# Group 1's triangular inversion moved to VectorE, and the opening of the recurrence emitted in another order

## The chip, the cores and the metric

The kernel runs on one core of one Trainium2 chip. The metric is the device time of one execution in microseconds (us); lower is better. Engines are named as in the profile: PE (TensorE's matmuls), DVE (VectorE), ACT (ScalarE), POOL (GpSimd) and SP (SyncE, which here issues most DMA transfers).

## The reference

Two layers of a diffusion transformer block over 512 latent and 256 context tokens of width 1024. Each layer projects the normed input; one part of the columns feeds a bidirectional RWKV recurrence of 8 heads of 64, the other a differential attention of 8 heads; their outputs are concatenated and projected, and a squared-ReLU MLP follows. What matters here is the recurrence:

```
def wkv_scan(state0, r, w, k, v, kk, b, reverse):
    xs = tuple(jnp.swapaxes(t.astype(jnp.float32), 0, 1) for t in (r, w, k, v, kk, b))

    def step(state, inp):
        r_t, w_t, k_t, v_t, kk_t, b_t = inp
        sa = jnp.einsum("bhvk,bhk->bhv", state, kk_t)
        state = (state * w_t[:, :, None, :]
                 - sa[..., :, None] * b_t[:, :, None, :]
                 + v_t[..., :, None] * k_t[:, :, None, :])
        y = jnp.einsum("bhvk,bhk->bhv", state, r_t)
        return state, y
```

It runs forward and backward, first over the context, then from the context's state over the latent tokens.

## The kernel before

The recurrence is computed in chunks of 64 tokens. Two chunks of 64 make a group of 128 tokens; there are 6 groups, and each is treated in both directions (d = 0 and 1) at once. Per group there are three kinds of work.

*Preparation.* `prep_a` and `prep_b` handle a unit of one group, one direction and half of the heads: 24 units per layer, in the order of the groups. A unit loads the projected columns (L973), makes decay and rate with a small matmul (L977) and a tanh on ACT (L982), doubles it to sg on POOL (L1014), takes a running sum over the chunk on DVE (L1018 forward, L1020 backward), exponentials on ACT, and writes scaled keys (BK, L1034 and L1035). Matmuls of these (L1046) are masked on DVE (L1048) into S, the chunk's matrices, and the keys are transposed (L1053). `preps()` gives out the units one after the other; when the fourth unit of a group is done, the group's number is put into `ready`.

*Inversion.* Each chunk's unit triangular 64x64 matrix has to be inverted. `relay` copies the two diagonal 32x32 blocks of every matrix to DRAM (L1086), `inv` loads them back as N and W (L1115, L1116), `eliminate` inverts all of a group's blocks together in 30 sweeps of one multiplication (L1100) and one addition (L1102) each, 60 instructions one behind the other, and after that the inverse goes out to DRAM as it is (dn, L1123) and transposed (dt, through R, L1125 and L1127), and back as TT (L1132) and into S (L1137). `merge` then makes the off-diagonal block with 32 small matmuls on PE (L1152, L1154), a copy Z on ACT, 32 more matmuls (L1160, L1162), and a copy into S on DVE (L1164) and one on ACT (L1165).

*Steps.* `step(n, j)` advances the recurrence by one chunk in both directions: it loads the values uv (L1176), multiplies keys and state into X (L1186, L1189), copies that to xs (L1192), solves with the inverse into us (L1198), updates the state with more matmuls (L1210) and two DVE instructions (L1213, L1215), and makes the output y (L1226). Every step needs the merged inverse of its group from L1198 on.

The attention of the layer (`phase_wr`: row maximum L797, exponential L799, scaling by the second softmax L809, transposes L815 and their copies L820, values L832, norm L843 and L848, store L858) runs while the first units are prepared. Its loop calls `side(1)` after its pieces, which emits the next piece of `prologue()`. What the prologue has not emitted when attention is through is drained by `rest()`, which then does merge(0), merge(1) and the steps, and between their parts emits the later groups' preparation and inversion and the rows of the adaptive norm for the rest of the layer (`ada`, weights loaded by L254 into raw, multiplied by L265).

The order on each engine is made by a scheduler at build time from the order of emission, dependences and its own estimates, so an instruction can stand before or behind its neighbours of emission. Each engine then works through its own order strictly: an instruction that waits holds up what is behind it. This holds for SP's transfers as well.

Before the change, groups 0 and 1 are eliminated on POOL (`n < 2`) and groups 2 to 5 on DVE, and the prologue emits all units of groups 0 and 1, then all of inv(0), then all of inv(1).

Of the kernel before, what the change touches and what calls it, by code (L numbers as in the profile page):

```python
# [10 lines left out]
F32 = mybir.dt.float32  # L11
# [153 lines left out]
class K:  # L165
# [760 lines left out]
    def recurrence(self, l, last, es, side):  # L926

        nc, tc, I, dr = self.nc, self.tc, self.I, self.dr
        tp = self.pool(es, "tp", 1)
        iv = self.pool(es, "iv", 1)  # L930
# [128 lines left out]
        def preps():  # L1059
            todo = [(n, d, pp) for n in range(6) for d in range(2) for pp in (0, 2)]  # L1060
            nxt = prep_a(*todo[0])
            for i, it in enumerate(todo):
                cur = nxt
                if i + 1 < len(todo):
                    nxt = prep_a(*todo[i + 1])
                yield
                yield from prep_b(*it, *cur)
                if it[1:] == (1, 2):
                    ready.append(it[0])
                    yield  # L1070

        ready, tts = [], {}
        prepg = preps()
# [15 lines left out]
        def base(d, bl):  # L1089
            b = (bl + d) % 2 * 32 + d * 16  # L1090
            return slice(b, b + 16)

        def eliminate(N, W, n):

            for t in range(1, 31):
                k, w = (t + 1) // 2, 31 - t
                pr = iv.tile([128, 128], F32, name=self.n("pr"), tag=f"pr{n < 2}")
                prv = pr[:, 0:k * w].rearrange("p (s j) -> p s j", s=k)
                ve = nc.gpsimd if n < 2 else nc.vector
                ve.tensor_tensor(prv, W[:, 0:k, t:t + 1].to_broadcast([128, k, w]),  # L1100
                                        N[:, t:t + 1, t + 1:32].to_broadcast([128, k, w]), ALU.mult)
                ve.tensor_tensor(W[:, 0:k, t + 1:32], W[:, 0:k, t + 1:32], prv, ALU.add)  # L1102
                if t % 4 == 0:
                    yield
            for par in range(2):
                nc.gpsimd.memset(W[64 * par:64 * par + 64].rearrange("p s t -> p (s t)")[:, par:512:34], 1.0)

        def inv(n):

            N = iv.tile([128, 32, 32], F32, name=self.n("N"), tag="N", bufs=2)  # L1110
            W = iv.tile([128, 16, 32], F32, name=self.n("W"), tag="W", bufs=2)
            da = das[n].rearrange("u (i r t) -> u i r t", r=2, t=32)
            for par in range(2):
                ps = slice(64 * par, 64 * par + 64)
                nc.sync.dma_start(W[ps], da[:, :, par])  # L1115
                nc.sync.dma_start(N[ps].rearrange("p s t -> p (s t)"), das[n])  # L1116
            yield
            yield from eliminate(N, W, n)
            dn = dr.tile([64, 1024], F32, name=self.n("dn"))
            dt_ = dr.tile([32, 2, 512], F32, name=self.n("dt"))  # L1120
            dv = dn.rearrange("u (i r t) -> u i r t", r=2, t=32)
            for par in range(2):
                nc.sync.dma_start(dv[:, :, par], W[64 * par:64 * par + 64])  # L1123
            R = iv.tile([128, 32, 16], F32, name=self.n("R"), tag="R")
            nc.scalar.copy(R, W.rearrange("p s t -> p t s"))  # L1125
            for par in range(2):
                nc.sync.dma_start(dt_[:, par], R[64 * par:64 * par + 32].rearrange("p t s -> p (t s)"))  # L1127
            yield
            Gs = [sets[(n, d)][2].rearrange("s u h t -> s (u h) t") for d in range(2)]
            TT = iv.tile([64, 16, 32], F32, name=self.n("TT"), tag="TT")  # L1130
            for d in range(2):
                nc.sync.dma_start(TT[32 * d:32 * d + 32].rearrange("t u (r i) -> t (u r) i", r=2),  # L1132
                                  dt_[16 * d:16 * d + 16].rearrange("u r (t i) -> t (u r) i", t=32))
            for d in range(2):
                for bl in range(2):
                    bs = slice(32 * bl, 32 * bl + 32)
                    nc.sync.dma_start(Gs[d][bs, :, bs], dn[base(d, bl), :].rearrange("u (s t) -> s u t", s=32))  # L1137
            tts[n] = TT
            yield
            if n > 1:  # L1140
                merge(n)
                yield

        def merge(n):
            TT = tts.pop(n)
            Gs = [sets[(n, d)][2].rearrange("s u h t -> s (u h) t") for d in range(2)]
            a, e = slice(0, 32), slice(32, 64)
            get = late.get("pg", bank)
            zps = get([64, 16, 32])
            Z = iv.tile([64, 16, 32], F32, name=self.n("Z"), tag="Z")  # L1150
            for u in range(16):
                nc.tensor.matmul(zps[e, u, :], Gs[0][a, u, 32:64], TT[a, u, :],  # L1152
                                 start=True, stop=True, skip_group_check=True)
                nc.tensor.matmul(zps[a, u, :], Gs[1][e, u, 0:32], TT[e, u, :],  # L1154
                                 start=True, stop=True, skip_group_check=True)

            nc.scalar.copy(Z.rearrange("p u (i r) -> p u r i", r=2), zps.rearrange("p u (r i) -> p u r i", r=2))
            nps = get([64, 16, 32])
            for u in range(16):
                nc.tensor.matmul(nps[a, u, :], Z[e, u, :], Gs[0][e, u, 32:64],  # L1160
                                 start=True, stop=True, skip_group_check=True)
                nc.tensor.matmul(nps[e, u, :], Z[a, u, :], Gs[1][a, u, 0:32],  # L1162
                                 start=True, stop=True, skip_group_check=True)
            nc.vector.tensor_copy(Gs[0][a, :, 32:64], nps[a])  # L1164
            nc.scalar.copy(Gs[1][e, :, 0:32], nps[e])  # L1165
# [130 lines left out]
            yield  # L1296

        def prologue():
            while 1 not in ready:
                yield next(prepg)  # L1300
            yield from inv(0)
            yield from inv(1)

        def rest():
            nonlocal uvp, fp, px, us, xsd
# [50 lines left out]
        done, spare = [], []  # L1356
        uvp = fp = px = us = xsd = None
        side.add(prologue())
        return rest

# [379 lines left out]
```

## Time and profile before

| | |
|---|---|
| median of 3 runs | 2432.26 us (2419.16 to 2433.48) |
| the profiled execution | 2426.55 us, its span 2424.8 us |
| busy share of the span: PE, DVE, ACT, POOL | 93%, 63%, 48%, 33% |
| mean granted clock of TensorE | 0.946 of 2.4 GHz |

The span is the time from the first to the last instruction; it is taken from one execution. Busy time counts the time in which an engine runs an instruction, and not its waits. A granted clock of 1.00 is the full clock of TensorE and 0.5 half of it; a mean over a stretch lies between. A timeline row gives the start, the duration, the engine, the line of the kernel, the operation, what it writes and reads, the count of instructions that it stands for, and in brackets the idle time of the engine before it with what ended it.

### The profile page before, as it was taken

The numbers are of one execution on the slowest core, as the hardware profiler recorded it, in microseconds if no ns is written. First come the engines' busy times: TensorE is split into PE (matmuls) and PEld (weight loads), VectorE is DVE, ScalarE is ACT, GpSimd is POOL, SyncE is SP. The second block draws the span as 40 slices with busy tenths as digits, with TensorE's granted clock in tenths as the row PEclk, the third lists the DMA queues.
The fourth block names the chain that finished last, engine by engine and source line by source line (L and its number), as shares of the span: only waits on it lengthen the run. The fifth ranks groups of instructions, "written<-read, shape, count | busy, mean of one in ns | idle before, by whom it ended". The sixth has DMA issues, their size and how long they took to land.

```text
span 2424.8 us, 43738 instructions
## 1 busy us (share of the span) xinstructions
PE 2250.5 (93%) x17150; PEld 1903.9 (79%) x17150; DVE 1518.5 (63%) x2629; ACT 1174.4 (48%) x2393; POOL 803.6 (33%) x1048
## 2 busy tenths in 40 slices
PE   6999998899988999999999999999879988999997
PEld 5887887787777988888888887778767877788886
DVE  5456458647755675555556736665856575778784
ACT  4345547545534544333344435555735544555552
POOL 1212324832212343333330422323562121553530
PEclk9999999779998999999999999999879988999999
DMA  7543445377577521111112344454567664423230
GB/s 275 157 131 87 122 126 134 81 207 186 148 190 221 196 92 60 64 61 62 61 63 85 136 137 133 115 144 110 115 171 198 153 181 161 165 88 121 86 114 35
DMA packets 291630, 313.67 MB, mean 129 GB/s; under 512 B 139680, under 2 KB 220896, under 8 KB 291424
## 3 DMA queue, kind: packets, MB, share of 16 engines
q1 hardware_dynamic: 280320, 284.66, 38.8%
q0 software_dynamic: 10240, 23.08, 5.0%
q8 instruction: 135, 2.21, 0.4%
q10 hardware_dynamic: 864, 3.15, 0.3%
q14 instruction: 71, 0.58, 0.1%
HBM read 257.04 MB, written 53.77 MB: 128 GB/s over the span
## 4 chain that ended last, share of the span: by engine, by line
PE 66%; DVE 10%; DMA 8%; issue 5%; POOL 4%; ACT 4%; SPq 2%; ACTq 0%; POOLq 0%; DVEq 0%
PE pf L351 32%; PE pu L351 16%; PE po L351 4%; DMA raw<-in_ada_w 2%; PE po L832 2%; PE pb L1046 2%; PE sc L795 1%; DVE wl L1500 1%; POOL pr L1100 1%; POOL W L1102 1%; PE X L1189 1%; DVE nm L797 1%; PE X L1226 1%; PE adar L265 1%; PE ptr L815 1%
## 5 line engine op out<-in xcount | busy, mean ns | idle before, releaser
L1500 DVE TENSOR_TENSOR wl<-raw,wh 128x1024 fp32r<-128x1024 f32 x170 | 255.8, 1507 | 125.0 <-ACT wh L1499 124.2
L351 PE MATMUL pf<-hl,wh 128*128 128x512 f32 (+1 forms) x832 | 282.1, 342 | 0.0
L351 PE MATMUL pf<-hh,wh 128*128 128x512 f32 (+1 forms) x832 | 280.5, 342 | 0.6 <-ACT hh L397 0.6
L351 PE MATMUL pf<-hh,wl 128*128 128x512 f32 (+1 forms) x832 | 275.7, 342 | 0.0
L1499 ACT ACTIVATE wh<-raw 128x1024 fp32r<-128x1024 f32 x170 | 179.2, 1058 | 161.5 <-PE pf L351 143.9
L351 PE MATMUL pf<-wh,fah 128*128 128x512 f32 x570 | 224.5, 396 | 13.2 <-DVE fu L1633 7.2
L351 PE MATMUL pu<-hh,wh 128*128 128x512 f32 (+1 forms) x632 | 223.7, 354 | 4.8 <-DVE t L557 1.7
L351 PE MATMUL pf<-wl,fah 128*128 128x512 f32 x570 | 223.9, 394 | 0.7 <-DVE wl L1500 0.7
L351 PE MATMUL pf<-wh,fal 128*128 128x512 f32 x570 | 221.4, 394 | 1.8 <-DVE fal L1600 1.8
L351 PE MATMUL pu<-hh,wl 128*128 128x512 f32 (+1 forms) x632 | 218.6, 346 | 4.0 <-DVE wl L340 4.0
L351 PE MATMUL pu<-hl,wh 128*128 128x512 f32 (+1 forms) x632 | 218.0, 345 | 0.0
L797 DVE TENSOR_REDUCE nm<-sc 128x1 f32<-128x768 f32 (+1 forms) x160 | 132.5, 841 | 79.3 <-PE sc L795 78.5
L351 PEld LDWEIGHTS pf<-hl,wh 128*128 128x128 f32 x832 | 156.6, 188 | 20.0 <-DVE hl L399 0.2
L351 PEld LDWEIGHTS pf<-hh,wl 128*128 128x128 f32 x832 | 156.1, 188 | 20.0
L351 PEld LDWEIGHTS pf<-hh,wh 128*128 128x128 f32 x832 | 155.3, 188 | 20.4 <-ACT hh L397 0.8
L799 ACT ACTIVATE e<-sc,nm 128x768 f32<-128x768 f32 (+1 forms) x160 | 130.7, 821 | 53.9 <-DVE nm L797 44.3
L321 POOL TENSOR_TENSOR rs<-ms,pw 128x1 f32<-128x1 f32 (+2 forms) x60 | 56.7, 948 | 271.2 <-DVE ms L319 270.5
L351 PEld LDWEIGHTS pu<-hh,wh 128*128 128x128 f32 x632 | 121.2, 192 | 23.4 <-DVE t L557 2.4
L351 PEld LDWEIGHTS pf<-wh,fah 128*128 128x128 f32 x570 | 107.2, 188 | 40.6 <-ACT fah L1599 13.6
L1633 DVE TENSOR_TENSOR acc<-pf,acc 128x512 f32<-128x512 f32 x155 | 104.2, 682 | 53.9 <-PE pf L351 53.3
L351 PEld LDWEIGHTS pu<-hh,wl 128*128 128x128 f32 x632 | 121.0, 192 | 19.0 <-DVE wl L340 4.8
L351 PEld LDWEIGHTS pu<-hl,wh 128*128 128x128 f32 x632 | 121.1, 192 | 14.3 <-issue 1.7
(262 smaller groups left out, 5607.1 us busy)
## 6 DMA issues: line engine op xcount, KB each, us to landing
raw<-in_w_ff SPq DMA_DIRECT2D x128, 512.0 KB, 3.7
raw<-in_ada_w SPq DMA_DIRECT2D x96, 512.0 KB, 6.5
raw<-in_w_in SPq DMA_DIRECT2D x52, 512.0 KB, 4.0
ld<-zd SPq DMA_DIRECT2D x40, 384.0 KB, 5.5
ks<-qd POOLq DMA_DIRECT2D x64, 192.0 KB, 5.4
zd<-zr SPq DMA_DIRECT2D x22, 384.0 KB
raw<-in_w_out SPq DMA_DIRECT2D x16, 512.0 KB, 5.9
qs<-qd POOLq DMA_DIRECT2D x32, 192.0 KB, 5.9
```

The source lines that it names most:

```text
L265: nc.tensor.matmul(acc[32 * g:32 * g + 32, :], self.sc[:, 2 * kp + k, :], raw[:, k, g * 128:g * 128 + 128], start=(kp + k == 0), stop=(kp ...
L321: nc.gpsimd.tensor_tensor(r, m, self.pw1.to_broadcast([128, cols]), ALU.pow)
L351: nc.tensor.matmul(out, a, b, start=(start and i == 0 and j == 0), stop=(i == n - 1 and j == 2), skip_group_check=not start)
L795: nc.tensor.matmul(sc[:, k0:k1], qs[:, br, tk], ks[:, br, k0:k1], start=True, stop=True)
L797: nc.vector.tensor_reduce(nm, sc, AX.X, ALU.max, negate=True)
L799: nc.scalar.activation(ee, sc, AF.Exp, bias=nm, accum_out=ls[:, br:br + 1])
L815: nc.tensor.transpose(pt[:, (k - k0) * 128:(k - k0) * 128 + 128], e[0][:, k * 128:k * 128 + 128], self.ident)
L832: nc.tensor.matmul(po, pT[:, k * 128:k * 128 + 128], vn[:, k, h * 64:h * 64 + 64], start=(k == 0), stop=(k == nk - 1))
L1046: nc.tensor.matmul(pgt[:, u, 0:nn], BK[hs, u, :], KR[hs, 2 * pp + u, 0:nn], start=True, stop=True, skip_group_check=True)
L1499: nc.scalar.activation(hi, src, AF.Copy)
L1500: nc.vector.tensor_tensor(lo, src, hi.bitcast(F32), sub)
L1633: nc.vector.tensor_tensor(d, p, d, add)
```

## The change

Two edits in `recurrence()`. In `eliminate`, group 1's 60 instructions go to DVE instead of POOL, and its products pr use the buffer of the later groups. In `prologue`, the units are emitted until group 0 is ready; then one piece of preparation and one piece of inv(0) are emitted by turns until group 1 is ready, and then pieces of inv(1) and inv(0) by turns.

```
@@ eliminate
-                pr = iv.tile([128, 128], F32, name=self.n("pr"), tag=f"pr{n < 2}")
+                pr = iv.tile([128, 128], F32, name=self.n("pr"), tag=f"pr{n == 0}")
                 prv = pr[:, 0:k * w].rearrange("p (s j) -> p s j", s=k)
-                ve = nc.gpsimd if n < 2 else nc.vector
+                ve = nc.gpsimd if n == 0 else nc.vector
@@ prologue
-            while 1 not in ready:
+            while 0 not in ready:
                 yield next(prepg)
-            yield from inv(0)
-            yield from inv(1)
+
+            first, second = inv(0), None
+            while first or second or 1 not in ready:
+                if 1 not in ready:
+                    next(prepg)
+                    if 1 in ready:
+                        second = inv(1)
+                elif second and next(second, self) is self:
+                    second = None
+                    continue
+                if first and next(first, self) is self:
+                    first = None
+                yield
```

How the engines' orders differ after it is shown at three places. The first is SP's order in layer 0 at the end of attention (od is its last store; uv are the values of step (0,0) in the two directions; dn, dt, TT and S with these numbers are group 1's inverse; gprow and raw belong to the adaptive norm). It is a piece of the difference, with + for rows that only the changed kernel has here.

```order
 L858 DMA od_522<-oT_5103 128x768
 L1176 DMA uv_5296<-vnd_521 64x512
+L1123 DMA dn_4905<-W_4704 1024x1x32 x2
 L1176 DMA uv_5298<-vnd_521 64x512
+L1127 DMA dt_4906<-R_4909 32x512 x2
+L1137 DMA S_4141<-dn_4905 32x16x32 x2
+L1132 DMA TT_4928<-dt_4906 32x32x16 x2
+L1137 DMA S_4484<-dn_4905 32x16x32 x2
 L306 DMA gprow_5315<-in_rows 128x256
 L254 DMA raw_5318<-in_ada_w 128x1024
```

The ten transfers of group 1's inverse moved from a later place in the queue to between and behind the two uv loads, ahead of the loads of in_ada_w.

The second is PE's order in layer 0, from the end of merge(1)'s first half (TT_4928, Z_5227 and pg_5226 are its tiles; X_5407 and us_5152 belong to step (0,0); adar to the adaptive norm). It is again a piece of the difference.

```order
+L1154 MATMUL pg_5226<-TT_4928,S_4484 32x32
+L1189 MATMUL X_5407<-sbd_3609,S_3914 128x128
+L1198 MATMUL us_5152<-xs_5130,S_3658 64x64 x8
+L1053 MATMUL pb_5544<-cst,BK_5526 128x128 x4
+L977 MATMUL pb_5554<-ltz_3602,wab_3600 128x256
 L265 MATMUL adar_5317<-raw_5318,sc 32x128 x8
-L1189 MATMUL X_5407<-sbd_3609,S_3914 128x128 x3
-L1198 MATMUL us_5152<-xs_5130,S_3658 64x64 x2
+L1160 MATMUL pg_5261<-S_4141,Z_5227 32x32
```

Merge(1) moved ahead: its first half stands before the last matmul of X and the solve of step (0,0), its second half behind the first L265; before, both stood behind step (0,1)'s X.

The third is DVE's order in layer 1 around merge(0)'s copy L1164 (W_17731 is group 1's block, W_18643 group 2's). Before:

```order
L1032 SCALAR_TENSOR_TENSOR ta_18915<-ta_18915,ld_18909 128x256
L1035 TENSOR_TENSOR BK_19010<-th_18914,xi_19004 128x4x64
L1034 TENSOR_TENSOR BK_19010<-ta_18915,xi_19004 128x4x64
L1164 COPY S_16631<-pg_18205 32x16x32
L309 TENSOR_TENSOR row_18709<-adar_18668,gprow_18666 128x128
L310 TENSOR_TENSOR row_18709<-row_18709,gprow_18666 128x128
L1100 TENSOR_TENSOR pr_18714<-W_18643,N_18642 128x30
```

In the changed kernel, DVE has there:

```order
L1102 TENSOR_TENSOR W_17731<-W_17731,pr_17935 128x15
L1100 TENSOR_TENSOR pr_18714<-W_18643,N_18642 128x30
L1102 TENSOR_TENSOR W_18643<-W_18643,pr_18714 128x30
L1100 TENSOR_TENSOR pr_18717<-W_18643,N_18642 128x29
L1102 TENSOR_TENSOR W_18643<-W_18643,pr_18717 128x29
L1100 TENSOR_TENSOR pr_18720<-W_18643,N_18642 128x56
L1102 TENSOR_TENSOR W_18643<-W_18643,pr_18720 128x2x28
L1100 TENSOR_TENSOR pr_18723<-W_18643,N_18642 128x54
L1102 TENSOR_TENSOR W_18643<-W_18643,pr_18723 128x2x27
L1164 COPY S_16631<-pg_18205 32x16x32
```

Ahead of the copy there stand now the last instructions of group 1's elimination and the first eight of group 2's, which used to stand behind it. Elsewhere in layer 1, counting the units of both layers from 0 (24 to 27 are layer 1's group 0): eleven instructions of group 1's elimination stand on DVE ahead of the mask (L1048) of unit 34; on PE the last L832 of attention stands ahead of L977 of unit 32, and used to stand behind that of unit 33; and on POOL sg (L1014) of unit 38 stands ahead of the last instruction of group 0's elimination, and used to stand behind it.

## Rows read from the trace of the kernel before

**Rows 1.** The page: busy time of each engine, and the ending chain by line.

```profile
PE 2250.5 (93%) x17150; PEld 1903.9 (79%) x17150; DVE 1518.5 (63%) x2629; ACT 1174.4 (48%) x2393; POOL 803.6 (33%) x1048
PE pf L351 32%; PE pu L351 16%; PE po L351 4%; DMA raw<-in_ada_w 2%; PE po L832 2%; PE pb L1046 2%; PE sc L795 1%; DVE wl L1500 1%; POOL pr L1100 1%; POOL W L1102 1%; PE X L1189 1%; DVE nm L797 1%; PE X L1226 1%; PE adar L265 1%; PE ptr L815 1%
```

**Rows 2.** Layer 0: window, length, busy time (instructions) by engine, PE clock, DMA share, GB/s.

```profile
520.00:540.00 20.00, 19.27 (x307) 15.83 (x306) 6.18 (x13) 5.72 (x13) 2.36 (x5) 0.66 0.89 197
```

**Rows 3.** Windows of layer 1; engines in the order PE, PEld, DVE, ACT, POOL.

```profile
1740.00:1800.00 60.00, 43.25 (x495) 34.05 (x493) 30.80 (x59) 24.03 (x59) 45.78 (x110) 0.71 0.69 167
1800.00:1860.00 60.00, 55.42 (x826) 45.08 (x826) 40.37 (x119) 30.09 (x74) 17.62 (x45) 0.87 0.77 194
```

**Rows 4.** Groups of instructions: busy us, mean ns of one, idle before and its releaser.

```profile
L1100 DVE TENSOR_TENSOR pr<-W,N 128x30 f32<-128x30 f32 (+7 forms) x240 | 67.6, 282 | 31.9 <-DMA N<-da 26.6
L1102 DVE TENSOR_TENSOR W<-W,pr 128x30 f32<-128x30 f32 (+7 forms) x240 | 65.2, 272 | 5.8
L1102 POOL TENSOR_TENSOR W<-W,pr 128x30 f32<-128x30 f32 (+7 forms) x120 | 48.2, 402 | 7.9
L1100 POOL TENSOR_TENSOR pr<-W,N 128x30 f32<-128x30 f32 (+7 forms) x120 | 47.1, 393 | 12.8 <-DMA N<-da 3.8 <-issue 1.8
```

**Rows 5.** Timeline of SP's queue in layer 0 (SPq issues transfers).

```profile
465.29 1.27 SPq L1123 DMA_DIRECT2D dn<-W  x2
...
490.40 1.38 SPq L254 DMA_DIRECT2D raw<-in_ada_w  x3
...
504.81 2.08 SPq L1123 DMA_DIRECT2D dn<-W  x2
```

**Rows 6.** Timeline of PE in layer 0.

```profile
472.37 0.31 PE L1152 MATMUL pg<-TT,S 32*32 32x32 f32 x2 [0.71 <-DMA TT<-dt]
...
500.64 0.64 PE L265 MATMUL adar<-raw,sc 128*32 128x128 f32 x16
...
502.08 0.34 PE L1198 MATMUL us<-xs,S 128*64 128x64 f32 x4
...
520.95 0.64 PE L265 MATMUL adar<-raw,sc 128*32 128x128 f32 x16 [0.73 <-DMA raw<-in_ada_w]
...
523.04 0.31 PE L1152 MATMUL pg<-TT,S 32*32 32x32 f32 x2
```

**Rows 7.** Timeline of POOL in both layers.

```profile
465.34 0.24 POOL L1100 TENSOR_TENSOR pr<-W,N 128x30 f32<-128x30 f32 x1
...
1776.18 0.23 POOL L1102 TENSOR_TENSOR W<-W,pr 128x15 f32<-128x15 f32 x1
...
1779.90 0.41 POOL L1014 TENSOR_SCALAR sg<-th 128x256 f32<-128x256 f32 x1
...
1810.26 0.23 POOL L1102 TENSOR_TENSOR W<-W,pr 128x15 f32<-128x15 f32 x1
```

**Rows 8.** Timeline of DVE in layer 0, at its gaps.

```profile
474.47 0.42 DVE L820 COPY pT<-ptr 128x256 f32<-128x256 f32 x1 [5.34 <-PE ptr L815]
...
480.61 0.95 DVE L843 TENSOR_REDUCE s<-osq 128x12 f32<-128x768 f32 x1 [5.72 <-ACT osq L841]
...
490.91 0.69 DVE L1048 TENSOR_TENSOR S<-pb,cst 128x512 f32<-128x512 f32 x1 [4.15 <-PE pb L1046]
```

**Rows 9.** Transfers issued from 480 to 530 us: count, size, median us to landing.

```profile
raw<-in_ada_w SPq DMA_DIRECT2D x10, 512.0 KB, 4.8
```

**Rows 10.** Timeline of DVE in layer 1.

```profile
1789.00 0.68 DVE L1164 COPY S<-pg 32x512 f32<-32x512 f32 x1 [5.48 <-PE pg L1162]
...
1795.71 0.40 DVE L1100 TENSOR_TENSOR pr<-W,N 128x30 f32<-128x30 f32 x1 [3.15 <-DMA N<-da]
```

**Rows 11.** Timeline of SP's queue in layer 1.

```profile
1788.92 0.67 SPq L1116 DMA_DIRECT2D N<-da  x1
```

**Rows 12.** Windows of L1100 alone: DVE and POOL busy (instructions), clock, DMA share, GB/s.

```profile
1795.00:1806.50 11.50, 4.95 (x12) 3.52 (x10) 0.53 0.35 112
1806.50:1823.40 16.90, 5.29 (x18) 1.32 (x5) 0.88 0.81 188
```

## The prediction

> **What bounds the kernel now.** The page comes first: PE is busy for 93% of the span, and the two lines of POOL's elimination stand in the chain that ended last with 1% each, beside matmul lines of up to 32% [rows 1]. So the kernel is a matmul kernel, and a change outside PE can pay only in stretches where PE idles or runs at the lower clock. Next the windows: each layer has one such stretch, where attention ends and the recurrence starts. In layer 0, PE is busy for 19.27 of the 20 us from 520 to 540, at a granted clock of 0.66, a mean of TensorE's two levels, 2.4 GHz (1.00) and 1.2 GHz (0.5) [rows 2]. I count the loss of a window as its length less busy time times clock: 20 - 19.27 x 0.66 = 7.3 us. In layer 1 it is 60 - 43.25 x 0.71 = 29.3 us from 1740 to 1800, and 60 - 55.42 x 0.87 = 11.8 us from 1800 to 1860 [rows 3]. That is the whole purse: 48.4 us, 2% of the span, and much of it belongs to attention's tail and to merge(0), which the change does not speed up.
>
> **What moves.** Each elimination is 30 multiplications (L1100) and 30 additions (L1102). On POOL they take 393 and 402 ns, so 30 x (0.393 + 0.402) = 23.8 us per group; on VectorE 282 and 272 ns, so 16.6 us [rows 4]. The change takes group 1's 60 instructions from POOL to VectorE in both layers: 120 x 0.277 = 33.2 us more on VectorE (busy 1518.5 us), 47.7 us less on POOL (803.6 us) [rows 1, 4]. Neither engine is the bound over the span, so totals decide nothing; what decides is when inverse 1 is ready and what queues behind it. The new order of emission itself moves little in layer 0: the scheduler had already put group 0's elimination on POOL between units that are emitted ahead of and behind it. It is priced by its effect in layer 1, below.
>
> **Layer 0, gain.** On POOL the two eliminations run one after the other: the first store of inverse 0 is issued at 465.29, that of inverse 1 at 504.81 [rows 5]. From the store to merge 0's first matmul it took 472.37 - 465.29 = 7.1 us, for merge 1, beside heavy transfers, 523.04 - 504.81 = 18.2 us [rows 5, 6]. N and W of group 1 are there by then, since POOL began on them at 465.34, right behind the first elimination and without a wait [rows 7]. On VectorE the order puts its 60 instructions into existing gaps: VectorE sat idle for 5.34 us before a copy at 474.47, 5.72 us before 480.61 and 4.15 us before a mask at 490.91 [rows 8]. Sixteen instructions need 16 x 0.277 = 4.4 us, so two groups of 16 fit the first two gaps and ten (2.8 us) the third; the last one stands behind the scan that follows that mask. The end comes at about 492.5 instead of 504.8. With merge 0's 7.1 us, merge 1 can start at about 500, and PE's new order has it ahead of us(0,0), whose first matmul was at 502.08 [rows 6]. So it costs no wait, or about 1 us if the chain is as slow as half the way to 18.2. Its matmuls are the same number, so PE's work between the ends of step (0,0) and (1,0) is unchanged. What goes away is the short wait and the low clock after 520: at 520.95 PE had sat idle for 0.73 us on a weight transfer, and the clock is low in the window that follows [rows 2, 6]. Up to 7.3 us come back.
>
> **Layer 0, loss.** The store of inverse 1 now stands in SP's queue between the two uv loads and ahead of the three loads of in_ada_w, and SP works in order. Those three went out at 490.40 [rows 5]; now they wait for the elimination's end (492.5) and for the loads of its two copies in DRAM (about 7 us more, as above), so they leave at about 501, 11 us later. They take 4.8 us to land [rows 9], so at 506 or later. Their first user, L265, ran at 500.64 [rows 6], and in the new order stands right behind us(0,0), which I put at 501 to 503. PE then waits for 3 to 5 us, and may go on at the low clock for a while. I take 4.3 us from the middle of it: -7.3 + 4.3 = **-3 us** in layer 0. The ends are -7 (the loads land in time) and, if the stall is 5 us and is followed by as much low clock as was after 520, -7.3 + 5 + 7.3 = +5.
>
> **Layer 1.** Here the order does change. Two units of group 2's preparation that stood on PE ahead of attention's end now stand behind it; that is the same work of PE, moved, so I price it at nothing. POOL's elimination of group 0 ended at 1776.41 (T from here), ahead of unit 38's sg (L1014), which went through POOL at 1779.90 [rows 7]. Now that sg stands ahead of the elimination's last instruction, so it ends at 1780 to 1782: T rises by about 5 us. On the other side group 1's elimination no longer waits for it: it ended at 1810.49 on POOL [rows 7], and now all its 60 instructions stand on VectorE ahead of merge 0's copy (L1164). Eleven of these, waiting for N of group 1, stand ahead of the mask of unit 34, and PE has work of that unit ahead of the first step's X; that load is issued early, so I price it at 0 to 3 us and take none. A new wait stands right ahead of L1164: eight instructions of group 2's elimination, which need N of group 2. Before, L1164 ran at 1789.00 and these at 1795.71, after 3.15 us idle on that load [rows 10]; the load was issued at 1788.92 [rows 11], so 6.8 us to start, and the order issues it now behind the loads of inverse 0, some 5 us after T. With T now about 1781, L1164 comes at T + 5 + 6.8 + 8 x 0.277 = T + 14, or T + 18 if the load is as late as one more such transfer. Before, it was at 1776.41 + 12.6. So step (0,0)'s solve begins at 1795 to 1799, 6 to 10 us later than before; I take 9. Against it: merge 1, whose inverse is done by about 1795 instead of 1810.5, no longer stops PE after 1800, where 11.8 us were lost [rows 3]; of that some 9 come back, the rest belonging to merge 2. Layer 1: +9 - 9 = **0**, between -10 (T does not rise, no wait on N) and +10 (the wait is paid and nothing comes back).
>
> **Two engines on one memory.** In layer 1 more of VectorE's elimination now runs beside POOL's. The trace shows this pair once: while POOL eliminated group 1 and VectorE group 2, twelve of VectorE's L1100 took 4.95 us, 0.41 each; in the stretch after, eighteen took 5.29, 0.29 each, while POOL's ten took 0.35 each beside it [rows 12], no more than its mean of 0.393 [rows 4]. So VectorE pays about 0.12 us per instruction and POOL nothing visible; for 40 shared instructions that is 4.8 us on an engine that is not the bound. The Trainium skill ("SBUF — State Buffer", section "SBUF: two separate sides") says that GpSimd and a VectorE operation with two SBUF inputs take their shared ports as an exclusive lock, the loser blocked for the whole instruction. By it POOL would be held up too, for the length of VectorE's instruction, which is the second rival. By the rows the sum gets nothing; by the rule it gets T + 8 to 11 us. The trace agrees on VectorE's side and not on POOL's.
>
> **The sum.** -3 + 0 gives 2426.55 - 3 = about 2424 us against the profiled execution's 2426.55. The three runs shown lie between 2419.16 and 2433.48 with a median of 2432.26, so that execution is 0.2% below the median, and my number is on its scale.
>
> **The rivals.** *The stretch heals* (chance 0.17): with merge 1 never late, PE in layer 1 has no idle time after 1800 and no low clock from it, T does not rise, and the loads of layer 0 land in time. For: the loss after the first merge [rows 2, 3] is 7.3 + 11.8 us. Against: T and L1164 stand later in the order. Price: -7.3 and -11.8, so about 2407. *Blocked ports make inverse 0 late* (0.12): if VectorE's instructions block POOL, 30 to 40 of them beside POOL's elimination of group 0 add 30 x 0.277 = 8.3 to 11.1 us to T in layer 1, and merge 0 is what PE waits for there. For: VectorE's own 0.12 us. Against: POOL's unchanged 0.35 us. It decides from the point where T passes 1785, since PE has run out of preparation by then; with the forecast's 9 us not regained it gives 2426.55 - 3 + 10 + 5 = about 2438. *Nothing happens* (0.09): since layer 0's POOL order was interleaved already and merge 1 was partly covered, both stretches only exchange one wait for another: 2426.5.
>
> **How the numbers follow.** The forecast, 2424, has 0.62, with its own range from -17 to +15 (both layers at their ends): 2409 to 2441. Taking the rivals in, 2405 to 2441 leaves about 0.1 out on either side. About 1%, 24 us, is what a measurement of this kernel can tell from no change. Below -24 lies only the deep end of the healing (0.09); above +24 only blocked ports together with a stall in layer 0 (0.05); within 1% is 0.86.
>
> **What the new profile would show.** Right, if in layer 0 merge 1's first matmul (L1152) is at about 500 with PE neither idle nor at a lower clock from 520 to 540, and a wait of 3 to 5 us on in_ada_w stands before L265; and if in layer 1 L1164 of merge 0 comes at 1795 to 1799 with VectorE idle before it on N. Wrong, if the in_ada_w loads land in time, if L1164 keeps its place relative to the last L1014, if POOL's L1100 grow longer than 0.393 us beside VectorE's, or if PE's losses from 1740 to 1860 fall by more than 10 us.

## The result

The changed kernel is slower. Four runs of it have a median of 2452.22 us (2449.25 to 2460.14), four of the kernel before 2428.0 us; the ratio is 1.0106, with a 95% interval from 1.0072 to 1.0140. The profiled executions have spans of 2447.5 and 2424.8 us, 22.7 us apart; every window and timeline below is of one profiled execution of its kernel.

First the page: the line of busy times of the changed kernel. The work moved, somewhat less of it than counted: 43 us off POOL (47.7 counted) and 26 us onto DVE (33.2 counted) [rows 1].

```profile
PE 2256.9 (92%) x17150; PEld 1912.1 (78%) x17150; DVE 1544.1 (63%) x2749; ACT 1174.5 (48%) x2393; POOL 760.3 (31%) x928
```

The groups of the two elimination lines in the changed kernel (busy us, mean ns of one, idle before) answer to [rows 4]. POOL's means are now those of group 0 alone, and are compared with group 0's of before further below:

```profile
L1100 DVE TENSOR_TENSOR pr<-W,N 128x120 f32<-128x120 f32 (+4 forms) x300 | 80.9, 270 | 34.3 <-DMA N<-da 25.9 <-DMA W<-da 0.9 <-issue 0.5
L1102 DVE TENSOR_TENSOR W<-W,pr 128x120 f32<-128x120 f32 (+4 forms) x300 | 80.0, 267 | 7.2
...
L1100 POOL TENSOR_TENSOR pr<-W,N 128x110 f32<-128x110 f32 (+20 forms) x60 | 25.1, 418 | 8.4 <-DMA N<-da 5.2
L1102 POOL TENSOR_TENSOR W<-W,pr 128x110 f32<-128x110 f32 (+20 forms) x60 | 25.0, 416 | 3.3
```

Then the windows of the changed kernel (window, length, busy of PE, PEld, DVE, ACT, POOL, granted clock, DMA share, GB/s); the first three answer to [rows 2, 3], the last is new:

```profile
520.00:540.00 20.00, 16.25 (x227) 13.44 (x225) 10.40 (x31) 8.03 (x21) 3.99 (x10) 0.91 0.78 210
...
1740.00:1800.00 60.00, 42.31 (x481) 33.36 (x480) 45.14 (x127) 25.02 (x62) 30.78 (x77) 0.73 0.75 181
1800.00:1860.00 60.00, 50.39 (x795) 43.34 (x796) 30.32 (x78) 28.70 (x72) 10.90 (x24) 0.80 0.60 146
1860.00:2020.00 160.00, 139.51 (x1893) 116.72 (x1892) 101.42 (x300) 74.31 (x168) 31.35 (x48) 0.83 0.66 170
```

and the same last window in the kernel before:

```profile
1860.00:2020.00 160.00, 147.78 (x2067) 125.66 (x2066) 106.39 (x294) 83.29 (x190) 34.52 (x52) 0.91 0.60 156
```

With the loss counted as in the prediction (length less busy time times clock), layer 0's window lost 5.2 us instead of 7.3. In layer 1, 1740 to 1800 lost 29.1 instead of 29.3, 1800 to 1860 lost 60 - 50.39 x 0.80 = 19.7 instead of 11.8, and 1860 to 2020 lost 160 - 139.51 x 0.83 = 44.2 instead of 25.5. So the change lost nothing where attention ends. It lost 8 us in the first steps of layer 1's recurrence and 19 us in its later ones, a stretch that the prediction did not look at. Of these 19 us, 8.3 are idle time of PE (160 - 139.51 = 20.5 us against 160 - 147.78 = 12.2), and the rest is busy time at the lower clock. The list of PE's waits from 1690 to 2030 (total us, times, longest) says what ended its idle time there. The kernel before:

```profile
PE us L1210 <- DVE st L1213: 8.5, 3, 5.2
PE pg L1152 <- DMA TT<-dt: 7.5, 5, 3.4
...
PE adar L265 <- DMA raw<-in_ada_w: 1.0, 2, 0.7
```

The changed kernel:

```profile
PE pg L1152 <- DMA TT<-dt: 16.2, 4, 7.6
PE adar L265 <- DMA raw<-in_ada_w: 15.9, 5, 7.6
```

The waits on the weights of the adaptive norm (in_ada_w) have grown from 1.0 to 15.9 us in layer 1, and those of merges on TT have doubled. The longest on TT, the two largest on the weights, and two other waits near the end stand in PE's timeline of the changed kernel:

```profile
1788.78 0.31 PE L1152 MATMUL pg<-TT,S 32*32 32x32 f32 x2 [7.55 <-DMA TT<-dt]
...
1828.21 1.08 PE L265 MATMUL adar<-raw,sc 128*32 128x128 f32 x16 [7.60 <-DMA raw<-in_ada_w]
...
1957.82 1.08 PE L265 MATMUL adar<-raw,sc 128*32 128x128 f32 x16 [4.74 <-DMA raw<-in_ada_w]
...
1993.96 1.13 PE L1281 MATMUL pb<-S,cst 128*128 128x512 f32 x2 [2.73 <-POOL S L1279]
...
2002.78 0.31 PE L1152 MATMUL pg<-TT,S 32*32 32x32 f32 x2 [4.13 <-DMA TT<-dt]
```

The wait of 7.55 us stands ahead of merge 0, in the window that loses no more than before. What the first wait on the weights (7.60 us) waited for stands in SP's queue of the changed kernel:

```profile
1808.29 1.53 SPq L254 DMA_DIRECT2D raw<-in_ada_w  x3
...
1815.40 1.26 SPq L1123 DMA_DIRECT2D dn<-W  x2
1816.75 2.33 SPq L1127 DMA_DIRECT2D dt<-R  x2
1820.49 0.32 SPq L1137 DMA_DIRECT2D S<-dn  x1
1820.91 1.03 SPq L1132 DMA_DIRECT2D TT<-dt  x2
...
1822.59 0.48 SPq L254 DMA_DIRECT2D raw<-in_ada_w  x1
```

Three loads of weights went out at 1808.29. The fourth stands behind the stores of inverse 2 (dn, 1815.40), which wait for the end of group 2's elimination, and behind loads (S, TT) that wait for those stores to land. It went out at 1822.59. In the kernel before, that same load stood ahead of the next inverse's stores:

```profile
1801.83 1.52 SPq L254 DMA_DIRECT2D raw<-in_ada_w  x3
...
1809.47 0.34 SPq L254 DMA_DIRECT2D raw<-in_ada_w  x1
1810.52 1.88 SPq L1123 DMA_DIRECT2D dn<-W  x2
```

### The profile page after: what moved, and what is told of

Same layout as the page of the kernel before. It is cut to its first block, busy times and chain, and to the rows that moved or that the text cites. A ratio compares the mean times of both kernels' runs of the same rounds, so it can differ in the third digit from the quotient of the medians.

```text
span 2447.5 us, 43765 instructions
## 1 busy us (share of the span) xinstructions
PE 2256.9 (92%) x17150; PEld 1912.1 (78%) x17150; DVE 1544.1 (63%) x2749; ACT 1174.5 (48%) x2393; POOL 760.3 (31%) x928
## 4 chain that ended last, share of the span: by engine, by line
PE 58%; DMA 7%; DVE 6%; ACT 3%; issue 2%; SPq 2%; POOL 1%; POOLq 0%; DVEq 0%; ACTq 0%
PE pf L351 31%; PE pu L351 7%; PE po L351 4%; PE pb L1046 2%; DMA raw<-in_ada_w 2%; PE pb L977 1%; PE adar L265 1%; PE X L1186 1%; PE po L832 1%; DVE wl L1511 1%; PE X L1189 1%; PE X L1226 1%; DMA TT<-dt 1%; PE us L1198 1%; PE us L1210 1%
```

## The experiments

Each figure behind "Measured" is the time of the run's kernel over that of the kernel before, with its 95% interval; a point is 1% of the time before, 24 us. Three theories were set against each other first. Theory 1: in layer 1 the early inverse 1 puts its transfers ahead of the weights' loads on SP, an effect of moving the elimination to VectorE. Theory 2: the new order of emission delays inverse 0 in layer 1. Theory 3: any edit makes the scheduler draw layer 1's order anew, and the time follows the draw.

**One edit at a time, one layer at a time (e1 to e4).** e1 has only the engine edit, e2 only the prologue, e3 both edits in layer 0 alone and e4 both in layer 1 alone.

```
# e1: the prologue of before, and in eliminate (pr's tag likewise)
-                ve = nc.gpsimd if n < 2 else nc.vector
+                ve = nc.gpsimd if n == 0 else nc.vector
# e2: the new prologue, eliminate and pr as before
# e3 (X = 0) and e4 (X = 1): eliminate, pr and prologue new where l == X
+                ve = nc.gpsimd if n < (1 if l == X else 2) else nc.vector
...
+            if l != X:
+                while 1 not in ready:
+                    yield next(prepg)
+                yield from inv(0)
+                yield from inv(1)
+                return
```

> Group 1's elimination on VectorE in both layers, the old order of emission. Theory 1 (in layer 1 the early inverse 1 puts its DRAM copies ahead of the loads of in_ada_w on SP, and merge 0 waits): about 18 to 24 us slower than before, all of it in layer 1, layer 0 about 4 us shorter. Theory 2 (the new order of emission delays inverse 0 in layer 1): about 4 us faster than before. Theory 3 (any edit makes the scheduler draw layer 1's order anew, and the time follows the draw): layer 0 about 4 us shorter as in the changed kernel, layer 1 anywhere from -10 to +30.

Measured: 1.0015 (0.9986 to 1.0043).

> The new order of emission in both layers, groups 0 and 1 both on POOL. In layer 0 the engines' orders are those of before, so all theories expect no difference there (within 1 us). Theory 1: within 5 us of before over all. Theory 2: about 20 to 25 us slower, all in layer 1. Theory 3: layer 1 anywhere from -10 to +30.

Measured: 1.0000 (0.9969 to 1.0032).

> Both edits in layer 0 alone; layer 1 has the program of before. Theories 1 and 2: layer 0 about 4 us shorter and layer 1 as before, so 2 to 5 us faster in all. Theory 3: layer 0 about 4 us shorter, but layer 1, whose order differs from before although nothing is edited there, moves by more than 5 us either way.

Measured: 1.0014 (0.9981 to 1.0047).

> Both edits in layer 1 alone; layer 0 has the program of before. Theories 1 and 2: layer 0 as before, layer 1 as in the changed kernel, so about 25 to 28 us slower. Theory 3: layer 0 as before, layer 1 differs from the changed kernel's by more than 5 us, since its order is another one.

Measured: 1.0035 (1.0008 to 1.0063).

Neither edit alone costs the 1.06%, so theories 1 and 2 fall as they were stated. Nor do both edits in layer 1, where all of the loss lay: e4 loses a third of it. e3 lies too near to 1 to tell the theories apart. The orders explain how that can be. In layer 0, e1's engines run in the changed kernel's order and e2's in that of before, but for a handful of rows: there the new emission does nothing. In layer 1 every one of the four has an order of its own, e3 too, whose layer 1 is not edited at all: going by the traces, at least 900 of PE's 6,900 rows and 60 of SP's 397 stand elsewhere than before. The scheduler simulates time, so a shift in layer 0 can reach layer 1.

**The order pinned (p0, p1, p2).** To vary the order and nothing else, the following kernels add an order-only dependence from each instruction to its predecessor on its engine, for a recorded order of all engines:

```
# shortened: the recorded orders are stored packed
+def pin(tc, nc):
+    ins = {i.name: i for i in nc.cur_bb.bb.instructions}
+    for order in PIN.values():
+        for a, b in zip(order, order[1:]):
+            tc.add_manual_dep(ins[b], ins[a].name, mybir.DependencyInfo(
+                mybir.DependencyClass.NoSync, mybir.DependencyReason.DATA), reason="pin")
```

p0 pins the changed kernel to its own order, a control. p1 has the same instructions, with layer 1 in the order that was drawn for e4. p2 is e3 with layer 1 in the order of before.

> The changed kernel with every engine's order pinned to the one it has anyway, a control for the runs in which one place of the order is altered. All theories: as the changed kernel, 0.7 to 1.4% slower than before.

Measured: 1.0100 (1.0038 to 1.0163).

> The changed kernel's instructions, both edits in both layers, with layer 0 in the changed kernel's order and layer 1 in the order that the scheduler drew for the kernel with the edits in layer 1 alone (e4). Theory 3 (the time follows the order drawn for layer 1, not the edits): within 12 us of before. If the edits themselves cost the time (theories 1 and 2): 20 us or more slower than before, like the changed kernel.

Measured: 1.0015 (0.9985 to 1.0045).

> Both edits in layer 0 alone, with layer 1 pinned to the very order of before, so that layer 0 is compared alone. The forecast's step for layer 0: 3 us faster than before, between 7 faster and 5 slower; layer 1's stretch the same length as before within 4 us. If layer 0's -2.5 us in the changed profile was the spread of one execution: no difference within 2 us.

Measured: 0.9993 (0.9961 to 1.0025).

The pinning costs nothing that shows. p1 settles the main question: the same instructions on the same engines, in another order for layer 1, take 0.85 points less. p0 has only four runs and a wide interval; with the changed kernel's own runs taken in, the difference is 0.90 points, give or take 0.4. The time lies in the drawn order, not in the edits as such; theory 3 holds. SP's queue of p1 shows what the other order does at the place of the longest wait on the weights:

```profile
1790.54 1.27 SPq L1123 DMA_DIRECT2D dn<-W  x2
...
1814.31 0.34 SPq L254 DMA_DIRECT2D raw<-in_ada_w  x1
...
1837.29 1.28 SPq L1123 DMA_DIRECT2D dn<-W  x2
```

Inverse 1 (1790.54) is early here too, with its elimination on VectorE, but the fourth load (1814.31) goes out 23 us ahead of inverse 2's stores (1837.29). p2 measures layer 0 alone: 0.07% faster than before, with an interval of 0.3% to either side. That agrees with the forecast's 3 us and with no difference.

**Which place of the order (p3 to p6).** All are p0 with single rows moved. Theory R says that the late weights cost the time; theory M that late merges do.

```
# SP, layer 1; p4 (and p6) has the first move alone, p3 all three
+L254 raw<-in_ada_w (fourth load of step (0,1))
 L1123 dn<-W (inverse 2) x2 ... S<-dn
-L254 raw<-in_ada_w (fourth load of step (0,1))
+L254 raw<-in_ada_w (4.74 us of wait at 1957.82)
 L1115 W<-da, L1116 N<-da (group 5) x4
-L254 raw<-in_ada_w (4.74 us of wait at 1957.82)
+L254 raw<-in_ada_w
 L973 ld, L970 ltz
-L254 raw<-in_ada_w
# DVE, layer 1; p5 and p6
+L1164 COPY S<-pg (merge 0)
 L1100, L1102 (group 2) x8
-L1164 COPY S<-pg (merge 0)
```

> The changed kernel, every engine pinned to its own order, but three loads of in_ada_w in layer 1 moved ahead on SP's queue: one ahead of the stores of inverse 2, one ahead of the loads of W and N of group 5, one ahead of three small loads. Theory R (these loads, late behind inverse transfers on SP, make PE wait 7.6, 4.7 and 2.4 us, and a stretch at half clock follows each): 12 to 20 us faster than the pinned kernel. Theory M (late merges cost the time, the loads only take up slack that the merges leave): less than 5 us faster.

Measured: 1.0044 (1.0016 to 1.0071).

> The pinned changed kernel with one load of in_ada_w alone, the fourth of step (0,1) in layer 1, moved ahead of the stores of inverse 2 on SP's queue. Theory R, one stall: the wait of 4.7 to 7.6 us before L265 goes, with half of the 10 to 14 us of half clock behind it: 9 to 14 us faster than the pinned kernel (ratio to before 1.004 to 1.006), as much as the three loads of p3 together, where a new wait of 7.7 us on L1213 stood in place of the last one. If all three loads mattered: 3 to 7 us faster.

Measured: 1.0041 (1.0016 to 1.0066).

> The pinned changed kernel with merge 0's copy L1164 in layer 1 moved ahead of the eight instructions of group 2's elimination that wait for N. The forecast's step (this wait costs 2.2 us of PE before us(0,0) and delays the rest): 2 to 6 us faster than the pinned kernel. Theory R alone, everything before the late load being made up later: less than 2 us.

Measured: 1.0086 (1.0057 to 1.0115).

> The pinned changed kernel with both moves of p4 and p5. If the two costs add: 11 to 20 us faster than the pinned kernel, within 0.5% of before. If merge 0's lateness is what makes the load late: no better than p4 alone, within 2 us.

Measured: 1.0051 (1.0028 to 1.0075).

One load of 512 KB, moved ahead on a queue, brings 0.59 points of the 1.00, some 14 us. With the changed kernel and p0 taken together it is 0.64 points, give or take 0.4. The queue of p4 and PE's timeline show it: the load goes out 0.4 us ahead of the stores of inverse 2, and L265 runs without a wait.

```profile
1819.11 0.35 SPq L254 DMA_DIRECT2D raw<-in_ada_w  x1
1819.54 2.13 SPq L1123 DMA_DIRECT2D dn<-W  x2
```

```profile
1823.11 0.64 PE L265 MATMUL adar<-raw,sc 128*32 128x128 f32 x16
```

Why more than the 7.6 us of the wait? The windows around it, in the changed kernel:

```profile
1814.00:1824.00 10.00, 5.25 (x121) 4.38 (x119) 3.21 (x11) 4.34 (x9) 0.44 (x3) 1.00 0.82 168
1824.00:1834.00 10.00, 5.79 (x49) 4.43 (x50) 0.26 (x1) 1.67 (x6) 0.40 (x1) 0.52 0.37 79
1834.00:1844.00 10.00, 10.00 (x105) 8.36 (x103) 7.63 (x14) 8.02 (x22) 3.62 (x8) 0.97 0.75 231
```

and in p4, at the same place of its program:

```profile
1816.00:1826.00 10.00, 8.67 (x170) 7.21 (x169) 3.71 (x13) 5.04 (x12) 0.44 (x3) 0.97 0.83 214
1826.00:1836.00 10.00, 9.73 (x111) 8.22 (x107) 7.53 (x14) 8.56 (x24) 3.67 (x8) 1.00 0.87 221
1836.00:1846.00 10.00, 10.00 (x216) 8.59 (x215) 7.61 (x16) 7.05 (x18) 3.33 (x7) 1.00 0.58 140
```

In the changed kernel PE was idle in the first two, and the granted clock is 0.52 in the second, half of full speed (1.2 of 2.4 GHz) for nearly all of it. The loss over the 30 us is 30 - (5.25 + 5.79 x 0.52 + 10 x 0.97) = 12.0 us, in p4 30 - (8.67 x 0.97 + 9.73 + 10) = 1.9 us. Of the 12.0 us, about 9 are idle time and 3 the lower clock. So the windows show 10 of the 14 us; the rest is within the interval.

p3 moved two more loads and gained no more than p4, though its own gain (0.56 points, 14 us) lies where theory R had it. The wait of 4.74 us did go, but the loads of W and N of group 5 were then behind, and VectorE stood before group 5's elimination, with the state of a step queued behind it. PE's timeline of p3:

```profile
1950.93 1.12 PE L1210 MATMUL us<-uv,S 128*64 128x64 f32 x16 [7.72 <-DVE st L1213]
```

and VectorE's:

```profile
1947.58 0.19 DVE L1100 TENSOR_TENSOR pr<-W,N 128x30 f32<-128x30 f32 x1 [7.90 <-DMA N<-da]
```

p5 leaves its question open: the eight instructions ahead of merge 0's copy, which the forecast priced, come out at 0.14 points, 3 us, with an interval that holds both nothing and the forecast's 2 to 6 us. p6, the better measure, is no better than p4 (0.10 points worse, give or take 0.35). No gain from an earlier merge 0 shows. Nor does the long wait on TT ahead of merge 0 cost what theory M would have it cost: p8, which comes below and is level with the kernel before, has it too, in PE's timeline:

```profile
1790.73 0.31 PE L1152 MATMUL pg<-TT,S 32*32 32x32 f32 x2 [8.69 <-DMA TT<-dt]
```

**A neighbouring wait in the kernel before (p7).** p2 with the state's instructions moved ahead of those that wait for N:

```
# DVE, layer 1, on top of p2
+L1213, L1215 (step (0,0), d = 0)
 L1100, L1102 (group 2) x4
+L1213, L1215 (step (0,0), d = 1)
 L1100, L1102 (group 2) x6
-L1213 ... -L1215 ... (d = 0, 1)
```

> Both edits in layer 0, layer 1 in the order of before (p2), with the state's two instructions L1213 and L1215 of step (0,0) on VectorE moved ahead of the first instructions of group 2's elimination, which wait for N there. If this wait is a cost of its own in the kernel before (PE idle 5.2 us before L1210, at half clock): 4 to 8 us faster than p2, 0.2 to 0.4% faster than before. If the next step has to wait for inverse 1 anyway (merge 1's first matmul at 1819.5 with 1.5 us of idle before it): within 2 us of p2.

Measured: 1.0009 (0.9976 to 1.0041), against p2's 0.9993. No gain shows for a wait of 5.2 us that the profile of before has in front of PE, though the two intervals do not exclude the first expectation's 4 us. In the profiles, PE's waits on the state (L1213) fell from 9.8 us in p2 to 4.6, and a wait of 4.7 us on in_ada_w appeared that p2 does not have. That merge 1 takes its place, as the second expectation has it, is not shown.

**The rest (p8 to p11).** p4 is behind the kernel before by 0.4% still. Its profile is about level with before at step (2,1) of layer 1 (2.8 us later) and 21 us later at step (5,1). So the order of the later steps was exchanged: p8 is p4 with the order of before from about step (2,1) on, p9 is p0 with that, and p10 is the kernel before with the changed kernel's order from there on. p11 is p8 in more runs.

```
# p8, p9 (A = changed, B = before) and p10 (A = before, B = changed), for each engine:
+    order = A's rows up to step (2,1) of layer 1 + B's rows behind it
```

> As p4 (the changed kernel with one load of in_ada_w moved ahead), but from about step (2,1) of layer 1 on every engine follows the order of before. If the remaining 0.4% of p4 lie in the order of layer 1's second half (p4's profile is 2.8 us behind before at step (2,1) and 21 us at step (5,1)): 8 to 14 us faster than p4, within 0.2% of before. If the second half is only late because the first half was: as p4, 0.3 to 0.5% slower than before.

Measured: 0.9976 (0.9946 to 1.0005).

> The changed kernel without the moved load, with the order of before from about step (2,1) of layer 1 on. If the load and the second half are costs that add: 8 to 14 us faster than the changed kernel, 0.4 to 0.6% slower than before. If the order of the second half costs only with the first half late: as the changed kernel, 0.8 to 1.1% slower than before.

Measured: 1.0048 (1.0012 to 1.0084).

> The kernel before, every engine pinned to its own order up to about step (2,1) of layer 1, and from there in the order of the changed kernel. If the order of the second half is a cost of its own: 0.3 to 0.6% slower than before. If it costs only behind the changed first half: within 0.2% of before.

Measured: 1.0041 (1.0014 to 1.0068).

> p8 once more, in more runs: the changed kernel with one load of in_ada_w moved ahead and layer 1's second half in the order of before. If the forecast's -3 us (0.12%) is what the edits are worth once the two costs are out: ratio to before 0.997 to 1.000. If p8's 0.9976 was the spread of its runs: 1.000 to 1.003.

Measured: 0.9996 (0.9971 to 1.0021).

These make a square:

| | later steps as changed | later steps as before |
|---|---|---|
| first steps as changed | p0 1.0100 | p9 1.0048 |
| the same, one load moved | p4 1.0041 | p8 0.9976, p11 0.9996 |

Down a column the load is worth 0.59 and 0.52 to 0.72 points, along a row the later steps 0.52 and 0.45 to 0.65; p10 finds 0.41 for the later steps behind the head of before. Each of these differences has an interval of 0.3 to 0.7 points to either side. With p0 and the changed kernel taken together, and p8 and p11, the load is worth 0.64 and 0.60 points and the later steps 0.57 and 0.53, each give or take 0.3 to 0.5. So far as that tells, the two costs add, and together they are the whole loss. With both out, the changed kernel can't be told from the kernel before; the forecast's -3 us is neither shown nor refuted by p8 and p11. The windows of p8 show where: 1860 to 2020 loses 160 - 145.49 x 0.95 = 21.8 us, against 44.2 in the changed kernel.

```profile
1860.00:2020.00 160.00, 145.49 (x2071) 122.77 (x2069) 108.08 (x298) 84.76 (x191) 35.53 (x52) 0.95 0.61 157
```

In p10's timeline of PE, the waits of the later steps are those of the changed kernel, on weights, on the finish of the outputs (S, L1279) and on inverse 5:

```profile
1958.67 0.71 PE L265 MATMUL adar<-raw,sc 128*32 128x128 f32 x16 [3.84 <-DMA raw<-in_ada_w]
...
1991.90 1.12 PE L1281 MATMUL pb<-S,cst 128*128 128x512 f32 x2 [2.73 <-POOL S L1279]
...
2000.51 0.31 PE L1152 MATMUL pg<-TT,S 32*32 32x32 f32 x2 [3.92 <-DMA TT<-dt]
```

Which of these three carries the 0.4 to 0.65% was not tried apart; in p3, moving the first one's load ahead of W and N gained nothing.

## Why the prediction was wrong

**The stage and its purse.** Right that only the two stretches around the start of the recurrence are open to the change, wrong where the second one ends. The loss was counted to 1860 and called the whole purse. The changed order reaches to the end of layer 1's recurrence, and 1860 to 2020 held 25.5 us of loss before and 44.2 after. What can be lost is not limited by what is lost now.

**Layer 0's gain.** Right in its steps. SP's queue and PE's timeline of the changed kernel:

```profile
488.84 1.69 SPq L1123 DMA_DIRECT2D dn<-W  x2
...
497.06 1.39 SPq L254 DMA_DIRECT2D raw<-in_ada_w  x3
```

```profile
496.62 0.31 PE L1152 MATMUL pg<-TT,S 32*32 32x32 f32 x2 [1.01 <-DMA TT<-dt]
...
500.58 1.12 PE L1198 MATMUL us<-xs,S 128*64 128x64 f32 x16
...
503.48 0.65 PE L265 MATMUL adar<-raw,sc 128*32 128x128 f32 x16
...
530.44 0.92 PE L265 MATMUL adar<-raw,sc 128*32 128x128 f32 x16 [3.75 <-DMA raw<-in_ada_w]
```

Inverse 1 left at 488.84, 3.7 us ahead of the estimated end of its elimination (492.5); merge 1 started 7.8 us later, for which 7.1 were taken, at 496.62 instead of 523.04 [rows 6], and us(0,0) was not held up (500.58, 502.08 before). But the window from 520 to 540 kept 5.2 of its 7.3 us of loss, with the clock at 0.91 and PE idle for 3.75 us at 530.44. The forecast had taken PE to be neither idle nor slow there.

**Layer 0's loss.** Right in size by luck. The three loads went out at 497.06 where 501 was expected, and L265 behind us(0,0) did not wait, so the stall that was priced did not come; the 3.75 us, inside the expected 3 to 5, came 27 us later on a later load, for which the forecast had no reason. The layer's sum of -3 us is met by p2's -0.07%, about -2 us, with an interval too wide to tell it from nothing.

**Layer 1, up to merge 0.** Right in times. POOL and VectorE of the changed kernel:

```profile
1779.16 0.54 POOL L1014 TENSOR_SCALAR sg<-th 128x256 f32<-128x256 f32 x1
1779.66 0.26 POOL L1102 TENSOR_TENSOR W<-W,pr 128x15 f32<-128x15 f32 x1
```

```profile
1793.68 0.19 DVE L1100 TENSOR_TENSOR pr<-W,N 128x30 f32<-128x30 f32 x1 [4.32 <-DMA N<-da]
...
1795.52 0.67 DVE L1164 COPY S<-pg 32x512 f32<-32x512 f32 x1
```

The elimination ended at 1779.92 (forecast 1780 to 1782), and L1164 came at 1795.52 (1795 to 1799), behind 4.32 us of idle on N. But the 9 us that were put down for it do not show as loss: 1740 to 1800 lost 29.1 us against 29.3 before, and with the wait on N gone, p5 and p6 gain no time that can be told from none.

**Layer 1, the rest: the step that failed.** "Of that some 9 come back" was the wrong sign. The stretch from 1800 to 1860 lost 19.7 us and not some 3. In this order group 2's elimination follows group 1's early one, and its inverse's transfers took the place on SP ahead of the fourth load of step (0,1). An early group 1 alone does not bring that about, as p1's queue shows. The prediction named this very mechanism in layer 0, in its own words that SP works in order, and followed the queue there. In layer 1 it followed the VectorE queue and left SP's out, though that order was at hand. The missing term is the load's 14 us. The other missing term, 10 to 16 us, is the order of the later steps: they were taken to be as before, while the changed kernel has over 1,000 of PE's rows of layer 1 elsewhere. Which wait among the later steps carries that term stays open.

**The rivals.** The rival on the slow side, blocked ports, named a cause that did not occur; that its 2438 us lies nearer to the measured time than the forecast is luck. In layer 1 the two eliminations ran beside each other from 1756 to 1780; the windows of L1100 and of L1102 alone in the changed kernel (DVE busy, POOL busy):

```profile
1756.00:1780.00 24.00, 4.82 (x15) 5.78 (x15) 0.86 0.83 246
...
1756.00:1780.00 24.00, 5.79 (x16) 5.85 (x15) 0.86 0.83 246
```

POOL's took 5.78 / 15 = 0.385 and 0.390 us, no longer than its means of before (0.393 and 0.402, [rows 4]). Like for like, the 30 multiplications and 30 additions of group 0 in layer 1 took 0.391 and 0.390 us each in the changed kernel, 0.404 and 0.412 before. The 418 and 416 ns of the groups above are means over both layers; in layer 0 group 0 took longer before as well (0.437 and 0.417, now 0.445 and 0.442), there with next to none of VectorE's elimination beside it. VectorE's took 0.32 and 0.36 us instead of 0.28 and 0.27. The Trainium skill ("SBUF — State Buffer", section "SBUF: two separate sides") has the loser of the shared ports blocked for a whole instruction. The trace agrees for VectorE and, in these instructions, not for POOL: T rose by 3.5 us to 1779.92, where the forecast had put it without such blocking, and not past 1785. The rival of no effect had an argument that held only for layer 0, as e2 showed. A chance of 0.05 for slower by over 1% was too low because the rivals were waits found in the order around one place, and the order changed in a thousand places.

## What to carry to other kernels

Where a scheduler places instructions by simulated times, a small edit is also a new draw of everything behind it, and the draw can outweigh the edit: here 0.85 points between two orders of the same instructions. Before judging such an edit, pin the order of what it doesn't touch (an order-only dependence along each engine), or time several draws. And when an inverse, a copy or any producer becomes ready earlier, follow the in-order issuing queue that its transfers share with loads: a wait at the head of that queue holds loads that have nothing to do with it, and PE pays for it in idle time and, here to a third as much, at half clock behind it.

## What the runs showed of the hardware

Executions of one and the same program differ more than the three runs shown at first: the kernel before took between 2412.09 and 2451.69 us in over a hundred runs on these chips, 1.6%, while the medians of its sets lie between 2428.0 and 2434.33. One profiled execution, or the difference of two, is no measure of 10 us: p2's profiled run took 2445.59 us against a median of 2427.9 for the same kernel.
